# Retention operands stacked by transfers, squares of three heads' norms folded to 64 rows, and the last pair's values taken from the back

## The chip, the cores and the metric

The kernel is written in Bass with the Tile framework and runs on one core of one Trainium2 chip, in one launch. Its metric is the device time in microseconds (us) of one execution. Before the change the median of three runs is 1220.32 us (1220.23 to 1221.1). Beside these there is one profiled execution, which took 1220.88 us; its profile spans 1219.1 us from the first to the last instruction.

The engines named below are PE (TensorE: matmuls and transposes), PEld (its weight loads), ACT (ScalarE), DVE (VectorE), POOL (GpSimd) and SP (SyncE, which here only issues transfers). Each engine runs its own instructions in their written order and waits on semaphores.

## The reference, cut to what matters

Two layers of an encoder over 512 tokens of width 1024, in float32. In each layer:

```
h = RMSNorm(x);  [rq|rk|rv|rg|dq|dk|dv] = h @ w_in
group A, retention, 8 heads of 64:  scores = (q k^T) * decay mask;  o = scores v + cross terms of the recurrent state
         ret = RMSNorm(o per head) * silu(rg)
group B, differential attention, 4 heads of 128:  a = softmax(q1 k1 + alibi) - lam * softmax(q2 k2 + alibi);  da = RMSNorm(a v per head)
x = x + concat(ret, da) @ w_out
x = x + (silu(RMSNorm(x) @ w_gate) * (RMSNorm(x) @ w_up)) @ w_down
```

RMSNorm of a head of group B divides by the root of the mean square over its 128 features; the features lie on the 128 partitions, so this sum runs across partitions and is made by a matmul with a matrix of ones.

## The kernel before, in words

All activations are held with features on partitions and the 512 tokens along the free dimension. A float32 operand is split into a rounded part (`hi`) and the rest (`lo`), both in the type fp32r; a product is then three fp32r matmuls, hi·hi, lo·hi and hi·lo (`mm3`, lines 208 to 210). The cast to `hi` is made by ACT, the subtraction that gives `lo` by DVE.

Each layer has these stages: the first projections (`project_first`, `project_dv`); the four heads of group B, each a generator (`diff_head`), with the remaining projections woven between them as fillers; then group A in four pairs of heads; then the output projection (`project_out`, half 0 for group B, half 1 for group A); then the feed-forward part, most of it in a fast product scheme (`seven`, line 867, from 331 us to 578 us of the span in layer 0), which the change does not touch.

**Group A.** The rows of a pair hold its two heads: partitions 0 to 63 (`ma`) are the first head's 64 features, 64 to 127 (`mb`) the second's. `prepare` (a0 to a3 in `STEPS`) builds, for each head, operands for scores in which both halves of the partitions carry something: `stack_one` makes `q`, with the rounded part on the head's own half and the rest on the other half; `stack_two` makes `khi`, with the rounded part on both halves, and `klo`, with the rest on one half and zeros (a POOL memset) on the other. So one score is two matmuls instead of three (line 536). Engines can write from one half to the other, 64 rows at a time: 2 ACT casts and 2 DVE subtractions for `q` (lines 358, 359), 4 ACT casts and 2 DVE subtractions for `k` (lines 367 to 369). `scores` (b0 to b3) makes the scores and multiplies them with the decays (DVE, line 541), which gives `sm`. `together` (k, v, V) issues a run of plain float32 matmuls: `state` (line 457), `cross` (`o<-wq,rs`, line 469) and `values` (`o<-sm,rv`, line 480). `norm` (n0 to n3) norms the pair and puts its split into `mix`.

**Norms of group B's heads.** `square_sums` squares the head's output (ACT, line 147), splits the squares into hi and lo (lines 226, 227), and issues two matmuls with ones (`aux<-hi,ones_r` line 140, `aux<-lo,ones_r` line 141).

**What sets the order.** `STEPS` is the order in which group A's steps are written; a "-" takes one step of the fillers (projections of the pairs 1 to 3, then the output projection's half 0, which copies each of its banks to `x` on ACT, line 724, and adds the old `x` by an accumulating POOL transfer, line 725). A scheduler then orders each engine's instructions from the written program. Weights come in by SP transfers (line 171) into three buffers; an SP transfer waits in SP's order until its buffer is free. PSUM has eight banks: two each of acc, sc, o and aux.

## Time and profile before

| | |
|---|---|
| median of three runs | 1220.32 us (1220.23 to 1221.1) |
| profiled execution | 1220.88 us, span 1219.1 us |
| PE busy | 1213.1 us, 100% of the span, 7637 matmul records |
| PEld busy | 1084.2 us, 89% |
| DVE busy | 971.3 us, 80% |
| ACT busy | 754.3 us, 62% |
| POOL busy | 93.8 us, 8% |
| granted PE clock | 1.000 |

How to read it: matmuls are pipelined, so a record of PE lasts longer than the time after which the next one starts. A matmul of 512 columns has a record of 0.39 us, while the next starts 0.23 us after it. The price of a matmul is therefore taken from start to start (called its slot below). The same holds for ACT and DVE, whose next instruction can start some 0.1 us before the record of the last one ends.

The stage that the change touches lies between 101 us of the span (the first squares of a head of group B) and some 253 us in layer 0; layer 1 repeats it 604.6 us later.

### The profile page before, as it was taken

How to read it: one execution, taken by the hardware profiler on the slowest of the kernel's cores; microseconds unless marked ns; L12 is line 12 of the kernel's file. 1: busy time of each engine (PE TensorE's matmuls, PEld its weight loads, DVE VectorE, ACT ScalarE, POOL GpSimd, SP SyncE). 2: the span in 40 equal slices, each digit the busy share in tenths (PEclk: the TensorE clock that was granted, in tenths of full speed). 3: DMA queues.
4: the chain of work that ended last, by engine and by line, in shares of the span. 5: the costliest groups of instructions: out<-in, count | busy, mean ns of one | idle time of the engine just before them, and what ended most of it. 6: DMA issues, size and time to landing. Idle time of an engine off the chain costs nothing.

```text
span 1219.1 us, 19925 instructions
## 1 busy us (share of the span) xinstructions
PE 1213.1 (100%) x7637; PEld 1084.2 (89%) x7637; DVE 971.3 (80%) x1601; ACT 754.3 (62%) x1316; POOL 93.8 (8%) x110
## 2 busy tenths in 40 slices
PE   9999999999999999999999999999999999999998
PEld 7888888878899999999888888887888999999997
DVE  6899778868978888886648997786789788898763
ACT  6877777755456656655548776785554565666551
POOL 1000000210011111110000000011100111111100
PEclk9999999999999999999999999999999999999999
DMA  7222221673166786782532222227532767867822
GB/s 267 87 70 74 83 69 53 138 191 104 57 164 166 177 210 158 177 219 90 168 112 79 77 70 70 85 66 163 138 119 67 184 146 188 207 161 181 203 78 95
DMA packets 67839, 158.83 MB, mean 130 GB/s; under 512 B 6176, under 2 KB 16672, under 8 KB 67744
## 3 DMA queue, kind: packets, MB, share of 16 engines
q1 hardware_dynamic: 50864, 127.75, 33.7%
q0 software_dynamic: 16448, 29.36, 14.8%
q8 instruction: 60, 0.98, 0.3%
q10 hardware_dynamic: 432, 0.44, 0.1%
q14 instruction: 35, 0.29, 0.1%
HBM read 153.34 MB, written 4.19 MB: 129 GB/s over the span
## 4 chain that ended last, share of the span: by engine, by line
PE 97%; ACT 2%; issue 0%; DMA 0%; DVE 0%; ACTq 0%
PE acc L867 23%; PE sc L867 17%; PE acc L208 10%; PE acc L209 10%; PE acc L210 10%; PE o L210 3%; PE o L209 3%; PE o L208 3%; PE sc L208 3%; PE sc L210 3%; PE sc L209 3%; PE sc L397 2%; PE o L480 1%; PE aux L413 1%; PE sc L536 1%; PE aux L140 1%
## 5 line engine op out<-in xcount | busy, mean ns | idle before, releaser
L195 ACT CAST hi<-raw 128x1024 fp32r<-128x1024 f32 (+2 forms) x117 | 115.8, 993 | 119.6 <-PE sc L209 39.3
L201 DVE TENSOR_TENSOR lo<-raw,hi 128x1024 fp32r<-128x1024 f32 (+2 forms) x118 | 135.2, 1150 | 45.5 <-ACT hi L195 44.7
L208 PE MATMUL acc<-h,hi 128*128 128x512 f32 (+1 forms) x344 | 133.8, 392 | 0.9 <-ACT h L219 0.9
L209 PE MATMUL acc<-h,hi 128*128 128x512 f32 (+1 forms) x344 | 134.2, 390 | 0.0
L210 PE MATMUL acc<-h,lo 128*128 128x512 f32 (+1 forms) x344 | 133.9, 389 | 0.0
L867 PE MATMUL acc<-hi,hi 128*128 128x256 f32 x432 | 122.5, 284 | 0.0
L867 PE MATMUL acc<-hi,lo 128*128 128x256 f32 x432 | 122.2, 283 | 0.0
L867 PE MATMUL acc<-lo,hi 128*128 128x256 f32 x432 | 122.2, 283 | 0.0
L824 DVE TENSOR_TENSOR lo<-s,hi 128x1024 fp32r<-128x1024 f32 (+1 forms) x78 | 89.0, 1141 | 32.7 <-ACT hi L823 32.4
L824 DVE TENSOR_TENSOR lo<-raw,hi 128x1024 fp32r<-128x1024 f32 (+1 forms) x78 | 89.0, 1141 | 30.5 <-ACT hi L823 26.9
L823 ACT CAST hi<-s 128x1024 fp32r<-128x1024 f32 (+1 forms) x78 | 76.6, 982 | 51.6 <-PE acc L867 37.1
L823 ACT CAST hi<-raw 128x1024 fp32r<-128x1024 f32 (+1 forms) x78 | 76.6, 981 | 39.0 <-PE acc L867 18.8
L867 PEld LDWEIGHTS acc<-lo,hi 128*128 128x128 f32 x432 | 82.9, 192 | 0.1
L867 PEld LDWEIGHTS acc<-hi,hi 128*128 128x128 f32 x432 | 82.9, 192 | 0.1
L867 PEld LDWEIGHTS acc<-hi,lo 128*128 128x128 f32 x432 | 82.9, 192 | 0.0
L208 PEld LDWEIGHTS acc<-h,hi 128*128 128x128 f32 x344 | 64.5, 188 | 15.1 <-ACT h L219 1.0
L210 PEld LDWEIGHTS acc<-h,lo 128*128 128x128 f32 x344 | 64.6, 188 | 13.3
L209 PEld LDWEIGHTS acc<-h,hi 128*128 128x128 f32 x344 | 64.7, 188 | 12.8
L845 POOL DMA_DIRECT2D s<-in_wgu x36 | 43.0, 1195 | 408.3 <-DMA s<-in_wgu 207.0
L867 PE MATMUL sc<-b,s 128*128 128x256 f32 x480 | 69.3, 283 | 0.0
L867 PEld LDWEIGHTS sc<-b,s 128*128 128x128 f32 x480 | 62.8, 192 | 0.0
L107 ACT ACTIVATE sc<-sc,mx 128x512 f32<-128x512 f32 x64 | 46.1, 720 | 20.2 <-DVE mx L401 20.1
(267 smaller groups left out, 3556.3 us busy)
## 6 DMA issues: line engine op xcount, KB each, us to landing
s<-in_wgu SPq DMA_DIRECT2D x54, 512.0 KB, 5.6
s<-in_wgu POOLq DMA_DIRECT2D x36, 512.0 KB, 7.9
raw<-in_wgu SPq DMA_DIRECT2D x34, 512.0 KB, 5.1
raw<-in_wsingle SPq DMA_DIRECT2D x32, 512.0 KB, 3.5
raw<-in_wvv SPq DMA_DIRECT2D x18, 512.0 KB, 3.5
raw<-in_wgu SPq DMA_DIRECT2D x36, 256.0 KB, 3.8
s<-in_wds SPq DMA_DIRECT2D x24, 384.0 KB, 3.4
raw<-in_wout SPq DMA_DIRECT2D x16, 512.0 KB, 4.3
```

Source lines behind the costliest of these rows:

```text
L107: i = nc.scalar.activation(out, src, f, **kw).ins
L140: sums[1] = nc.tensor.matmul(ps, w, hi, start=True, stop=False).ins.name
L195: c = nc.scalar.copy(hi[:, s], raw[:, s])
L201: nc.vector.tensor_tensor(lo[:, s], raw[:, s], f32(hi[:, s]), op=ALU.subtract)
L208: first = nc.tensor.matmul(out, L[0], R[0], start=start, stop=False)
L209: nc.tensor.matmul(out, L[0], R[1], start=False, stop=False)
L210: nc.tensor.matmul(out, L[1], R[0], start=False, stop=stop)
L397: nc.tensor.matmul(ps, q[m][:, t], k[m][part], start=part == 0, stop=part == 1)
L823: last_cast[0] = nc.scalar.copy(hi, raw).ins.name
L824: last_split[0] = nc.vector.tensor_tensor(lo, raw, f32(hi), op=ALU.subtract).ins.name
L845: nc.gpsimd.dma_start(sums, blocks[:, 0::3], accum_op=ALU.add)
L867: mm = nc.tensor.matmul(ps[:, t], L[x1], R[x2], start=start and k + i == 0, stop=k == n // P - 1 and i == 2, skip_group_check=True)
```

## The change

Four edits.

1. **Stacks by transfers.** In `prepare`, `moved_one` and `moved_two` take the place of `stack_one` and `stack_two`. The rounded part and the rest of both heads are made at once on 128 rows; for one of the two operands a cast of 64 rows follows; what has to lie on the other half of the partitions is moved there by SP transfers of 64 rows x 512 (128 KB): two for `q`, three for `k`. Per pair ACT has 4 casts (two of 128 rows, two of 64) instead of 6 of 64 rows, and DVE 2 subtractions of 128 rows instead of 4 of 64. The stacks of group B (`qk_tile`) stay as they were.
2. **Folded squares.** For the heads 0 to 2 of group B, `fold` squares the output and then adds the upper 64 rows onto the lower 64 by an accumulating POOL transfer. After a step of the generator, `folded_sums` rounds the 64 rows (ACT), writes the rest to the other 64 rows of the same tile (DVE), and one matmul with ones sums both. Head 3 keeps `square_sums`. The generator has one step more, and `heads` takes it one filler later.
3. **Values from the back.** The values of pair 3 are written from the last block and the second head to the first block and the first head; `stop` is False on all of them.
4. **Order.** In `STEPS`, b1 stands after k0+k1 instead of after a1, and the first matmul of the run k0+k1 is ordered behind the last score matmul written before it (`scored`).

```diff
@@ -35,7 +35,7 @@
 PLAIN = FFN[0][1]
 BEGUN, LASTS = (2, 9, 10, 20, 21), (18,)
 
-STEPS = "a0 h - b0 - a1 b1 - - - - k0+k1 - - a2 - - a3 V0+v1+k2+k3 b2 b3 n0 n1 - - - V2 n2 - - v3 - n3"
+STEPS = "a0 h - b0 - a1 - - - - k0+k1 b1 - - a2 - - a3 V0+v1+k2+k3 b2 b3 n0 n1 - - - V2 n2 - - v3 - n3"
 
 
 NW, NQK, NMIX, NAH, NHL = 12, 11, 20, 4, 3
@@ -147,6 +147,19 @@
         nc.scalar.activation(sq, src, AF.Square)
         column_sums(ps, w, sq)
         return sq
+
+    def fold(src):
+
+        sq = big("sq")
+        nc.scalar.activation(sq, src, AF.Square)
+        nc.gpsimd.dma_start(sq[:HD], sq[HD:], accum_op=ALU.add)
+        return sq
+
+    def folded_sums(ps, w, sq):
+        parts = big("hl", F32R)
+        nc.scalar.copy(parts[:HD], sq[:HD])
+        nc.vector.tensor_tensor(parts[HD:], sq[:HD], f32(parts[:HD]), op=ALU.subtract)
+        nc.tensor.matmul(ps, w, parts, start=True, stop=True)
 
     def round_ones():
         o = big("ones")
@@ -351,6 +364,28 @@
 
 
         ma, mb = slice(0, HD), slice(HD, P)
+
+        def moved_one(u, tag, bufs):
+            a, b = [big("q", F32R, tag, bufs) for _ in range(2)]
+            lo = big("qlo", F32R)
+            nc.scalar.copy(a, u)
+            nc.vector.tensor_tensor(lo, u, f32(a), op=ALU.subtract)
+            nc.scalar.copy(b[mb], u[mb])
+            nc.sync.dma_start(f32(a[mb]), f32(lo[ma]))
+            nc.sync.dma_start(f32(b[ma]), f32(lo[mb]))
+            return [a, b]
+
+        def moved_two(u, tag, bufs):
+            (ha, la), (hb, lb) = [(big("khi", F32R, tag, bufs), big("klo", F32R, tag, bufs)) for _ in range(2)]
+            nc.gpsimd.memset(f32(lb[ma]), 0.0)
+            nc.scalar.copy(ha, u)
+            nc.vector.tensor_tensor(la, u, f32(ha), op=ALU.subtract)
+            nc.scalar.copy(hb[mb], u[mb])
+            nc.sync.dma_start(f32(hb[ma]), f32(hb[mb]))
+            nc.sync.dma_start(f32(ha[mb]), f32(ha[ma]))
+            nc.sync.dma_start(f32(lb[mb]), f32(la[mb]))
+            nc.gpsimd.memset(f32(la[mb]), 0.0)
+            return [(ha, la), (hb, lb)]
 
         def stack_one(u, tag, bufs):
             q = [big("q", F32R, tag, bufs) for _ in range(2)]
@@ -422,8 +457,14 @@
                     vv = cut(v[hd // 2][j], slice(None), slice((hd % 2) * P, (hd % 2 + 1) * P))
                     mm3(o[:, th * C : (th + 1) * C], vv, (ah[:, j, :], al[:, j, :]), j == 0, j == 3)
                 yield
-            ss = aux_bank()
-            sq = square_sums(ss, consts["ones_r"], o)
+            if hd < DH - 1:
+                sq = fold(o)
+                yield
+                ss = aux_bank()
+                folded_sums(ss, consts["ones_r"], sq)
+            else:
+                ss = aux_bank()
+                sq = square_sums(ss, consts["ones_r"], o)
             rsqrt(sq, ss, 1.0 / P)
             nc.vector.scalar_tensor_tensor(sq, o, gd[:, l : l + 1], sq, op0=ALU.mult, op1=ALU.mult)
             mix[4 + hd] = split(sq, "mix", NMIX)
@@ -438,12 +479,16 @@
             for i, before in zip(ins, [names] + [[i.name] for i in ins]):
                 for name in before:
                     tc.add_manual_dep(i, name, order, reason="one run of plain matmuls")
+            if steps[0][0] == "k":
+                tc.add_manual_dep(ins[0], scored[0], order, reason="one run of plain matmuls")
             run[:] = ins[-1].name, ins[0].name
             first = [ret[int(t[1])]["weigh"] for t in steps if t[0] == "V"][:1]
             for i in first:
                 for name in names:
                     if name != i.name:
                         tc.add_manual_dep(i, name, order, reason="one run of plain matmuls")
+
+        scored = [None]
 
         def state(pr):
             kw, kv, ins = ret[pr]["kw"], aux_bank(), []
@@ -472,9 +517,9 @@
 
         def values(pr):
             o, s, ins = ret[pr]["o"], ret[pr]["s"], []
-            for c in range(2):
+            for c in ((1, 0) if pr == 3 else (0, 1)):
                 for j in range(2):
-                    for hh in range(2):
+                    for hh in ((1, 0) if pr == 3 else (0, 1)):
                         b = slice(hh * HD, (hh + 1) * HD)
                         ins.append(
                             nc.tensor.matmul(
@@ -482,7 +527,7 @@
                                 rv[pr // 2][2 * c + j][:, (pr % 2) * P + hh * HD : (pr % 2) * P + (hh + 1) * HD],
                                 s[c][:, hh, (1 - j) * C : (2 - j) * C],
                                 start=False,
-                                stop=(c == 1 and j == 1),
+                                stop=False,
                                 skip_group_check=True,
                             ).ins
                         )
@@ -509,7 +554,7 @@
                 op=ALU.mult,
             )
             ret[pr].update(qw=qw, kw=kw, state=[i.ins.name])
-            ret[pr]["stacks"] = stack_one(qT, "mix", NMIX), stack_two(kT, "mix", NMIX)
+            ret[pr]["stacks"] = moved_one(qT, "mix", NMIX), moved_two(kT, "mix", NMIX)
 
         def scores(pr):
             lgc = lambda d, hh: lg[:, l * 16 + d * 8 + 2 * pr + hh : l * 16 + d * 8 + 2 * pr + hh + 1]
@@ -536,6 +581,7 @@
                             i = nc.tensor.matmul(out, ks[hh][part][:, sb], qs[hh][:, tb], start=part == 0, stop=part == 1)
                             if run[0]:
                                 tc.add_manual_dep(i.ins, run[0], order, reason="one run of plain matmuls")
+                scored[0] = i.ins.name
                 sm = tpool.tile([P, 2, T], F32, tag="ah", name=nm("sm"), bufs=NAH)
                 for hh in range(2):
                     i = nc.vector.tensor_tensor(
@@ -668,7 +714,7 @@
                 for i in range(4):
                     next(head)
                     yield
-                    if i == 1 and late:
+                    if i in (1, 3) and late:
                         next(late)
                 late = head
             lasthead.append(late)
```

The built order moves at three places of each layer; layer 0 is shown. Numbers behind names are those of buffers.

**ACT, at the casts of the pairs 1 and 2** (q and khi are stacks of a pair, arg and wq its decays, raw and hi a weight and its rounded part, x the copy of an output bank). Before, the last rows of this stretch:

```order
L367 CAST khi_2152<-rk_2063 64x512
L369 CAST khi_2152<-rk_2063 64x512
L195 CAST hi_2505<-raw_2503 128x1024
L724 COPY x_2418<-acc_2405 128x512
L107 ACTIVATE wq_2224<-cst_sb,lg 128x256 x2
```

Behind the change, from pair 1's first cast:

```order
L371 CAST q_1842<-rq_1798 128x512
L373 CAST q_1843<-rq_1798 64x512
L381 CAST khi_1850<-rk_1731 128x512
L567 ACTIVATE arg_2030<-cst_sb,prm_sb 128x384
L567 ACTIVATE arg_2034<-cst_sb,prm_sb 128x384
L107 ACTIVATE wq_2130<-cst_sb,lg 128x256 x2
L383 CAST khi_1852<-rk_1731 64x512
L371 CAST q_2141<-rq_2097 128x512
L373 CAST q_2142<-rq_2097 64x512
L381 CAST khi_2149<-rk_2064 128x512
L770 COPY x_2423<-acc_2410 128x512
```

Before, twelve casts of 64 rows of two pairs and a weight cast stand ahead of the first copy; now there are seven casts, four of them of 128 rows, and decays (arg, wq); the weight cast stands behind the copy.

**PE, at the last pair's values** (o is the pair's bank, wq/rs the cross products, sm the weighted scores, the products with sc the output projection's second half, aux the sums of an earlier pair's norm). Before:

```order
L480 MATMUL o_2525<-sm_2349,rv_1899 64x256 x2
L480 MATMUL o_2525<-sm_2349,rv_1900 64x256 x2
L480 MATMUL o_2525<-sm_2362,rv_1901 64x256
L208 MATMUL sc_2613<-hi_2378,hi_2609 128x512
L209 MATMUL sc_2613<-lo_2379,hi_2609 128x512
L210 MATMUL sc_2613<-hi_2378,lo_2610 128x512
L208 MATMUL sc_2613<-hi_2395,hi_2609 128x512
L209 MATMUL sc_2613<-lo_2396,hi_2609 128x512
L210 MATMUL sc_2613<-hi_2395,lo_2610 128x512
L140 MATMUL aux_2470<-hi_2473,bones_r 128x512
L480 MATMUL o_2525<-sm_2362,rv_1901 64x256
L480 MATMUL o_2525<-sm_2362,rv_1902 64x256 x2
```

Behind the change:

```order
L514 MATMUL o_2530<-wq_2227,rs_373 128x256 x2
L140 MATMUL aux_2475<-hi_2478,bones_r 128x512
L221 MATMUL sc_2618<-hi_2383,hi_2614 128x512
L222 MATMUL sc_2618<-lo_2384,hi_2614 128x512
L223 MATMUL sc_2618<-hi_2383,lo_2615 128x512
L221 MATMUL sc_2618<-hi_2400,hi_2614 128x512
L525 MATMUL o_2530<-sm_2367,rv_1868 64x256 x2
L525 MATMUL o_2530<-sm_2367,rv_1869 64x256 x2
L525 MATMUL o_2530<-sm_2354,rv_1866 64x256 x2
L525 MATMUL o_2530<-sm_2354,rv_1867 64x256 x2
```

Before, the two cross products stood directly ahead of the first row shown, and the values were parted behind the fifth; now all eight stand together, and four products and a sum stand between them and the cross products.

**SP, at the stacks of the pairs 0 and 1.** Before, the loads of the output projection's weights followed each other here without anything between. Behind the change:

```order
L384 DMA khi_1705<-khi_1705 64x512
L385 DMA khi_1703<-khi_1703 64x512
L386 DMA klo_1706<-klo_1704 64x512
L374 DMA q_1695<-qlo_1697 64x512
L375 DMA q_1696<-qlo_1697 64x512
L184 DMA raw_2612<-in_wout 128x1024
L184 DMA raw_2638<-in_wout 128x1024
L374 DMA q_1842<-qlo_1844 64x512
L375 DMA q_1843<-qlo_1844 64x512
L385 DMA khi_1850<-khi_1850 64x512
L384 DMA khi_1852<-khi_1852 64x512
L386 DMA klo_1853<-klo_1851 64x512
```

The transfers of pair 0 and pair 1 stand ahead of and behind two weight loads; those of the pairs 2 and 3 follow, with two more loads between them.

## The prediction

> **What bounds the kernel now.** I read the page first, then the waits of PE, then the stretch around group A in order of time.
>
> The page:
>
> ```profile
> span 1219.1 us, 19925 instructions
> PE 1213.1 (100%) x7637; PEld 1084.2 (89%) x7637; DVE 971.3 (80%) x1601; ACT 754.3 (62%) x1316; POOL 93.8 (8%) x110
> ...
> PE 97%; ACT 2%; issue 0%; DMA 0%; DVE 0%; ACTq 0%
> ```
>
> PE is busy for 1213 of 1219 us and holds 97% of the chain of waits, at full clock (PEclk is 9 in every slice). What an engine beside PE saves is worth nothing unless PE waits for it. The view of PE's waits has three entries, 2.6 us together; the change touches only this one:
>
> ```profile
> PE acc L208 <- ACT x L724: 0.9, 2, 0.5
> ```
>
> So there are three ways to gain: fewer matmuls, that wait, and slots that are longer than they need be.
>
> **The wait.** In order of time, ACT and PE of layer 0, then PE of layer 1:
>
> ```profile
> 202.08 0.62 ACT L226 CAST hi<-sq 128x512 fp32r<-128x512 f32 x1
> 202.60 1.26 ACT L358 CAST q<-rq 64x512 fp32r<-64x512 f32 x2
> 203.88 0.62 ACT L367 CAST khi<-rk 64x512 fp32r<-64x512 f32 x1
> ...
> 206.46 1.26 ACT L358 CAST q<-rq 64x512 fp32r<-64x512 f32 x2
> ...
> 210.31 1.05 ACT L195 CAST hi<-raw 128x1024 fp32r<-128x1024 f32 x1
> 211.27 0.58 ACT L724 COPY x<-acc 128x512 f32<-128x512 f32 x1
> 211.75 0.91 ACT L107 ACTIVATE wq<-cst_sb,lg 128x256 f32<-128x256 f32 x2
> 212.56 1.11 ACT L522 ACTIVATE arg<-cst_sb,prm_sb 128x384 f32<-128x384 f32 x2
> 213.57 1.04 ACT L195 CAST hi<-raw 128x1024 fp32r<-128x1024 f32 x1
> ```
>
> ```profile
> 211.09 0.28 PE L536 MATMUL sc<-q,khi 128*128 128x256 f32 x1
> 211.22 0.28 PE L536 MATMUL sc<-q,klo 128*128 128x256 f32 x1
> 211.90 0.50 PE L208 MATMUL acc<-hi,hi 128*128 128x512 f32 x1 [0.41 <-ACT x L724]
> 212.23 0.39 PE L209 MATMUL acc<-lo,hi 128*128 128x512 f32 x1
> ...
> 815.80 0.28 PE L536 MATMUL sc<-q,klo 128*128 128x256 f32 x1
> 816.54 0.50 PE L208 MATMUL acc<-hi,hi 128*128 128x512 f32 x1 [0.46 <-ACT x L724]
> ```
>
> PE needs a bank that ACT's copy must empty, and the copy stands behind twelve narrow casts of the pairs 1 and 2. A 128-row cast lets the next start after 0.52 us (202.08 to 202.60), a 64-row cast only after 0.64 us (203.88 to 206.46: four in 2.58 us). Layer 0 loses 0.68 less a slot of 0.12 (211.09 to 211.22, rounded), 0.56 us, and 0.10 us more on the next slot (0.33 for 0.23); layer 1 loses 0.74 less 0.12, 0.62 us, and I take the same 0.10.
>
> In the changed order of ACT (shown with the change, from pair 1's casts to the copy that frees the same bank) there stand ahead of the copy four wide casts (2.08), three narrow ones (1.92), the two arg (1.01, from 212.56 to 213.57) and the two wq (0.81, from 211.75 to 212.56): 5.8 us. If this row of casts begins at 202.60 as before, the copy begins at 208.4 instead of 211.27 and ends at 209.0. PE comes to that bank just behind pair 1's first score. That score has 9 matmuls of 512 columns and 4 transposes more ahead of it than before (counted in the order): 9 x 0.23 + 4 x 0.11 = 2.5 us behind this row:
>
> ```profile
> 207.10 0.37 PE L536 MATMUL sc<-q,khi 128*128 128x256 f32 x1
> 207.30 0.60 PE L503 MATMUL aux<-cst_sb,rk 128*128 128x128 f32 x4
> ```
>
> So it starts at 209.6 instead of 207.10. PE asks for the bank at 209.7, which is then free for 0.7 us. First term: -(0.66 + 0.72) = **-1.4 us**; if the copy is as late as ever, 0.
>
> **The folded sums.** Six times one matmul goes. Its slot, from the timeline:
>
> ```profile
> 252.08 0.40 PE L141 MATMUL aux<-lo,bones_r 128*128 128x512 f32 x1
> 252.32 0.39 PE L208 MATMUL acc<-hi,hi 128*128 128x512 f32 x1
> ```
>
> 0.24 us, so 6 x 0.24 = **-1.4 us**; it is sure, since PE streams without a hole there. ACT and DVE have a cast and a subtraction as before. What is added is the accumulating transfer (128 KB), between these two rows of head 1:
>
> ```profile
> 141.62 0.60 ACT L147 ACTIVATE sq<-o 128x512 f32<-128x512 f32 x1 [0.72 <-PE o L210]
> ...
> 147.12 0.40 PE L140 MATMUL aux<-hi,ones_r 128*128 128x512 f32 x1
> ```
>
> The 64-row cast now stands in ACT's order behind one eviction, two weight casts and two exps: some 3.8 us busy; with the idle time that this stretch had (5.5 us from square to sum), 4 to 5 us. Bounds for the transfer are in the table of transfers:
>
> ```profile
> s<-in_wgu POOLq DMA_DIRECT2D x36, 512.0 KB, 7.9
> ...
> raw<-in_wds SPq DMA_DIRECT2D x16, 192.0 KB, 2.6
> ...
> x<-in_xT POOLq DMA_DIRECT2D x8, 256.0 KB, 4.9
> ...
> out_T<-x SPq DMA_DIRECT2D x1, 128.0 KB, 1.7
> ```
>
> Accumulating POOL transfers land after 4.9 us (256 KB) and 7.9 us (512 KB); half the smaller size should be under 4.9, and I take 4. Heads 0 and 2 have more behind the square (ten instructions or more). No cost.
>
> **The last pair's values.** PE's order is shown with the change. The eight values were cut into five and three; now they are whole, and the cut lies behind the two cross products. The times of pair 2 (a whole run) and pair 3:
>
> ```profile
> 239.66 1.03 PE L469 MATMUL o<-wq,rs 128*128 128x256 f32 x4
> 240.61 1.95 PE L480 MATMUL o<-sm,rv 128*64 128x256 f32 x16
> 242.49 0.39 PE L536 MATMUL sc<-q,khi 128*128 128x256 f32 x1
> 242.71 0.28 PE L536 MATMUL sc<-q,klo 128*128 128x256 f32 x1
> ...
> 243.54 1.03 PE L469 MATMUL o<-wq,rs 128*128 128x256 f32 x4
> 244.50 1.51 PE L480 MATMUL o<-sm,rv 128*64 128x256 f32 x10
> 245.94 0.50 PE L208 MATMUL sc<-hi,hi 128*128 128x512 f32 x1
> ...
> 247.43 0.40 PE L140 MATMUL aux<-hi,bones_r 128*128 128x512 f32 x1
> 247.76 1.08 PE L480 MATMUL o<-sm,rv 128*64 128x256 f32 x6
> 248.76 0.50 PE L208 MATMUL sc<-hi,hi 128*128 128x512 f32 x1
> 249.10 0.40 PE L209 MATMUL sc<-lo,hi 128*128 128x512 f32 x1
> ```
>
> Whole: 242.49 - 239.66 = 2.83, and 0.10 on the next slot: 2.93 us. Cut in five and three: 2.40 + 1.00, 0.10 on entering (247.43 to 247.76) and 0.11 on leaving (248.76 to 249.10), taken twice: 3.72 us. The cut costs 0.79 us: two heads' values run side by side (16 records in 1.88 us), and an odd one runs alone. Cut behind the cross products: 0.95 + 0.11, then 0.10 + 1.88 + 0.11 = 3.15 us. Gain 0.57 a layer, both layers **-1.1 us**; between -0.9 (another 0.1 at the new cut) and -1.6 (the new cut free). The Trainium skill (TensorEngine Tiling (Array Packing), Key Properties) says that changing the tiling mode drains the engine, and names no other cause. By it the cross products, which are of full width, would be left for free, and the gain would be 0.68 a layer. The trace does not agree that only the tiling counts: at 207.10 a score of full width takes 0.20 us for 0.12 ahead of transposes of full width, so a change between fp32r and plain float32 costs 0.08 us too.
>
> **The stacks' transfers.** 20 a layer on SP (its order in layer 0 is shown with the change). ACT saves 1.5 us a pair (six narrow casts against two of each kind) and DVE two subtractions, which is worth only the first term. Who may wait for the transfers is PE, at the scores. Pair 0's scores now come behind 46 matmuls of 512 columns, 12 of 256 and 8 transposes more: 12.7 us later, ample. Pair 2's scores come 19.6 us and pair 3's 27.9 us of slots behind pair 1's. Tight is pair 1: its last cast (khi_1852) ends at 202.60 + 0.52 + 0.64 + 0.52 + 1.01 + 0.81 + 0.62 = 206.7, and PE asks for it at 209.6 + 0.12 + 2 x 0.23 = 210.2. The transfer of khi_1850 waits for DVE's subtraction, which I put at about the same time, and PE asks for it at 209.6. So they may take 3.0 us. A store of 128 KB takes 1.7, a load of 192 KB 2.6; I take 2.0, nearest to the row of the same size. At the upper end, 4.9, PE waits 1.9 us a layer, +3.8 us. SP holds weight loads behind these transfers: the loads after pair 0's are read from 213.57 on (above), and go out near 194 by the same sums, so that even 7.9 us of landing leaves 11 us. POOL has 8 narrow memsets a layer as before; pair 1's last one follows its third transfer, and the scores that need it come 3.3 us of slots behind the first.
>
> **Sum.** -1.4 - 1.4 - 1.1 = -3.9 us on 1220.88 us: 1217.0. The median lies 0.6 us under the profiled execution, so the forecast is **1216.4 us**.
>
> **Rivals.**
> - *The wait only moves.* The copy's lead of 0.7 us is small, and another bank's copy or an operand of the pairs 1 to 3 may be late instead. For it: the same ACT order feeds them all. Against: 2.9 us are gained there. Then the first term is 0: 1220.3 - 2.5 = 1217.8.
> - *Pair 1's stacks come late.* Landing 4.9 instead of 2.0: 1216.4 + 3.8 = 1220.2. For it: loads and accumulations in the table are that slow. Against: they read from HBM and are larger.
> - *The folds hold ACT (slower).* ACT takes its instructions in order; if the folded rows land later than the 64-row cast's turn, the exps behind it wait, and PE's transposes behind those. At 7.9 us head 1's cast comes 4 us late and head 2's some 2 us (5.7 us of busy ACT stand behind its square): 6 us a layer, 12 in all if PE feels everything, 6 if half; the kernel is slower once PE feels over 3.2 us a layer. Time 1222.4 to 1228.4, say 1225. Against: 7.9 belongs to 512 KB.
> - *The change doesn't do what it says.* The order shows six matmuls fewer and the values whole; only the stacks could be without effect, which is the first rival.
>
> **Chances.** Forecast 0.60; the wait moves 0.14; pair 1 late 0.18; folds hold ACT 0.08. A measurement of this kernel tells about 0.2% (2.4 us) from no change: under 1217.9 is faster, over 1222.8 slower. Faster: 0.60 and half of the second (1217.8 is at the border) 0.67; slower 0.07, within 0.26. The range goes from 1215.2 (the new cut free, -0.5; two scores a layer no longer stand between transposes, 0.08 us each, -0.3; the rest rounding) to 1220.4 (pair 1 late): it leaves out the slower case and tails.
>
> **What would show it.** Right: PE's waits have no entry on the copy to x; six records of a single `hl,ones_r` matmul; the last values as 16 records in 1.9 us; stack transfers near 2 us. Wrong: a wait of PE at pair 1's scores on a transfer, idle time of ACT in front of the 64-row cast `hl` ended by a transfer, or new gaps of PE on DVE at pair 3.

## The result, and the profile after

The changed kernel takes **1216.57 us** in the median of six runs (1216.24 to 1216.87), the kernel before 1220.41 us (1220.23 to 1221.1) beside it. The ratio is 0.9967, 95% interval 0.9956 to 0.9978: faster by 3.8 us. The forecast was 1216.4 us.

The page of the changed kernel and the view of PE's waits (line, what it waited for: us, times, longest):

```profile
span 1214.5 us, 19995 instructions
PE 1210.0 (100%) x7631; PEld 1083.2 (89%) x7631; DVE 961.1 (79%) x1585; ACT 744.8 (61%) x1300; POOL 99.2 (8%) x116
```

```profile
PE aux L118 <- PEq L1165: 0.8, 1, 0.8
PE acc L221 <- ACT h L232: 0.4, 1, 0.4
```

PE has six records fewer, 7631, and its wait on the copy to `x` is gone. What is left lies in the start-up, as before. PE still is the bound: 1210.0 of 1214.5 us.

ACT and PE of the changed kernel in order of time, around the copy to `x` (L770 here):

```profile
200.52 1.06 ACT L208 CAST hi<-raw 128x1024 fp32r<-128x1024 f32 x1 [1.82 <-PE acc L222]
...
201.99 0.62 ACT L371 CAST q<-rq 128x512 fp32r<-128x512 f32 x1
...
208.20 0.58 ACT L770 COPY x<-acc 128x512 f32<-128x512 f32 x1
...
210.29 1.04 ACT L208 CAST hi<-raw 128x1024 fp32r<-128x1024 f32 x1
...
208.25 1.03 PE L548 MATMUL aux<-cst_sb,rk 128*128 128x128 f32 x8
209.04 0.36 PE L581 MATMUL sc<-q,khi 128*128 128x256 f32 x1
209.24 0.40 PE L221 MATMUL acc<-hi,hi 128*128 128x512 f32 x1
```

The copy begins at 208.20, right behind the last cast ahead of it, and ends at 208.78; PE takes the bank at 209.24. The order of casts worked out ahead of the run gave 208.4, 209.0 and 209.7.

One thing about this order was said wrongly with the change. The weight cast that stood between the narrow casts and the copy (at 210.31 before) does not stand behind the copy now. Counted in ACT's order it is the 35th of 195 weight casts (`hi<-raw`) in both kernels, and in the changed kernel the 35th is the row at 200.52, ahead of pair 1's casts, which begin no later for it (201.99, for 202.60 before). The row behind the copy, at 210.29, is the 36th, which stood behind the copy before too (213.57). So the row of ACT from pair 1's first cast to the copy is 208.20 - 201.99 = 6.2 us for 211.27 - 202.60 = 8.7 us before, and 0.96 us of the difference is this weight cast.

The last pair, in the same kernel's order of time on PE:

```profile
241.72 1.03 PE L514 MATMUL o<-wq,rs 128*128 128x256 f32 x4
242.40 0.58 PE L140 MATMUL aux<-hi,bones_r 128*128 128x512 f32 x1
242.82 0.39 PE L221 MATMUL sc<-hi,hi 128*128 128x512 f32 x1
...
243.83 1.95 PE L525 MATMUL o<-sm,rv 128*64 128x256 f32 x16
245.71 0.50 PE L221 MATMUL sc<-hi,hi 128*128 128x512 f32 x1
...
247.91 0.40 PE L140 MATMUL aux<-hi,bones_r 128*128 128x512 f32 x1
```

The eight values (16 records) run whole in 1.88 us. From the cross products to the sum of the last norm (the second L140) PE does the same work as before, both with 14 matmuls of 512 columns between: 247.91 - 241.72 = 6.19 us, where the kernel before took 250.47 - 243.54 = 6.93 us. That is 0.74 us a layer.

The table of transfers of the changed kernel (KB each, median us from issue to landing):

```profile
khi<-khi SPq DMA_DIRECT2D x16, 128.0 KB, 3.0
q<-qlo SPq DMA_DIRECT2D x16, 128.0 KB, 4.1
klo<-klo SPq DMA_DIRECT2D x8, 128.0 KB, 3.6
sq<-sq POOLq DMA_DIRECT2D x6, 128.0 KB, 2.9
```

The stacks' transfers take 3.0 to 4.1 us, not 2.0; the accumulating one 2.9, not 4.

Where the time went, by PE's records: "layer 0" runs from the first projected product to the first product of the feed-forward part with seven products, "layer 1" from there to the same product of layer 1. In the profiled executions of before they take 325.21 and 604.64 us, of after 323.11 and 602.77: -2.10 and -1.87. The start-up is 0.46 us shorter (6.04 to 5.58), the end 0.16, together 4.6 us of span. The medians differ by 3.8 only; the start-up comes back below.

### The profile page after: what moved, and what is told of

Same layout as the page of the kernel before. It is cut to its first block, busy times and chain, and to the rows that moved or that the text cites. A ratio compares the mean times of both kernels' runs of the same rounds, so it can differ in the third digit from the quotient of the medians.

```text
span 1214.5 us, 19995 instructions
## 1 busy us (share of the span) xinstructions
PE 1210.0 (100%) x7631; PEld 1083.2 (89%) x7631; DVE 961.1 (79%) x1585; ACT 744.8 (61%) x1300; POOL 99.2 (8%) x116
## 4 chain that ended last, share of the span: by engine, by line
PE 99%; DMA 0%; ACT 0%; DVE 0%; issue 0%
PE acc L913 23%; PE sc L913 17%; PE acc L221 11%; PE acc L222 11%; PE acc L223 11%; PE o L223 3%; PE o L222 3%; PE o L221 3%; PE sc L221 3%; PE sc L222 3%; PE sc L223 3%; PE sc L432 2%; PE sc L581 1%; PE o L525 1%; PE aux L448 1%; PE aux L140 1%
```

## The experiments

The intervals of the ratios are some 0.1% wide to each side, over 1 us, and most parts are worth no more than that. So each kernel is read by its two stages against those of before, and by the rows that changed; the medians are given beside them.

**One part alone.** The kernel before with one edit each.

`back_only`, the values from the back:

```diff
-            for c in range(2):
+            for c in ((1, 0) if pr == 3 else (0, 1)):
                 for j in range(2):
-                    for hh in range(2):
+                    for hh in ((1, 0) if pr == 3 else (0, 1)):
...
-                                stop=(c == 1 and j == 1),
+                                stop=False,
```

> The kernel before with the last pair's values from the back alone; stacks, norms and the order of steps as before. The built order has the two cross products, seven fp32r matmuls, then the eight values whole, in both layers; all else as before. Theory of the prediction (new cut at 0.11 + 0.10 a layer): 0.57 us a layer, 1220.4 - 1.1 = 1219.3. New cut almost free, as the trace of the changed kernel shows it (crosses 0.68 + 0.19 + 0.09, values 1.88 + 0.11): 0.77 a layer, 1220.4 - 1.5 = 1218.9. Rival, that the end of the values was hidden by DVE or ACT work and the gain comes back behind it: 1220.4. The wait of PE on ACT's copy to x (0.9, 2 times) stays under all three.

Measured: 1220.32 us beside 1220.7, ratio 0.9997 (0.9989 to 1.0006); stages -0.15 and -0.12. The rival is right: nearly all of the gain comes back. A new entry in PE's waits and the place in layer 0:

```profile
PE aux L140 <- ACT hi L226: 0.7, 2, 0.4
```

```profile
243.35 1.03 PE L469 MATMUL o<-wq,rs 128*128 128x256 f32 x4
...
249.31 0.40 PE L210 MATMUL sc<-hi,lo 128*128 128x512 f32 x1
250.06 0.50 PE L140 MATMUL aux<-hi,bones_r 128*128 128x512 f32 x1 [0.36 <-ACT hi L226]
250.40 0.39 PE L208 MATMUL acc<-hi,hi 128*128 128x512 f32 x1
```

Up to the sum PE would need 6.19 us, as in the changed kernel. But the slot from 249.31 to 250.06 is 0.52 us too long, the next one 0.10. So 0.62 of 0.74 us goes back. The sum waits for ACT's cast of the squares. ACT in this kernel, then in the changed kernel:

```profile
247.93 0.60 ACT L147 ACTIVATE sq<-o 128x512 f32<-128x512 f32 x1 [4.26 <-PE o L480]
248.82 0.69 ACT L107 ACTIVATE sq<-aux,eps_sb 128x512 f32<-128x512 f32 x1 [0.29 <-PE aux L141]
249.40 0.61 ACT L226 CAST hi<-sq 128x512 fp32r<-128x512 f32 x1
```

```profile
245.83 0.60 ACT L147 ACTIVATE sq<-o 128x512 f32<-128x512 f32 x1 [3.34 <-PE o L525]
246.46 0.62 ACT L239 CAST hi<-sq 128x512 fp32r<-128x512 f32 x1
```

In `back_only` alone a step of the earlier pair's norm (`sq<-aux`), which itself waits for PE's sum, stands between the square and its cast, so the cast ends at 250.01. In the changed kernel the cast follows the square and ends at 247.08, 0.83 us before PE needs it. An estimate from these rows: with the changed kernel's order the cast would end 1.25 us behind the square's start, at 249.18, and PE asks at 249.54, so the gain would have stayed. The number of matmuls between the values and the sum (seven here, nine there) is not what decides.

`fold_only`, the folded sums:

```diff
-            ss = aux_bank()
-            sq = square_sums(ss, consts["ones_r"], o)
+            if hd < DH - 1:
+                sq = fold(o)
+                yield
+                ss = aux_bank()
+                folded_sums(ss, consts["ones_r"], sq)
+            else:
+                ss = aux_bank()
+                sq = square_sums(ss, consts["ones_r"], o)
...
-                    if i == 1 and late:
+                    if i in (1, 3) and late:
```

> The kernel before with the folded sums of three heads alone. Its built order differs in two more places: the weight cast of 1024 columns that stood between the twelve narrow casts and the copy to x now stands behind the copy (about 0.96 us earlier for the copy), and PE comes to the copy's bank behind all eight scores of pair 1; and the last pair's values are cut in 4, 1 and 3 in place of 5 and 3 (one cut more, some 0.2 us a layer, +0.4). Theory A, the one of the prediction (the number of narrow casts makes the copy late, only the moved stacks remove the wait): six slots of 0.24 less, the wait stays, 1220.4 - 1.4 + 0.4 = 1219.4. Rival B (the wait was due to the place of that weight cast and of the scores, which the fold moves): 1220.4 - 1.4 - 1.4 + 0.4 = 1218.0, and PE's waits have no entry on the copy to x. Rival C (the folds hold ACT): 1220.4 or more, with ACT idle ahead of the cast hl.

Measured: 1219.11 us beside 1220.7, ratio 0.9988 (0.9979 to 0.9997); stages -0.74 and -0.61. PE's waits have no entry on the copy to `x` (L743 here). ACT, then PE at that place, then PE at the last pair:

```profile
200.86 1.05 ACT L208 CAST hi<-raw 128x1024 fp32r<-128x1024 f32 x1
...
209.93 0.57 ACT L743 COPY x<-acc 128x512 f32<-128x512 f32 x1
210.53 1.05 ACT L208 CAST hi<-raw 128x1024 fp32r<-128x1024 f32 x1
...
210.29 0.28 PE L555 MATMUL sc<-q,klo 128*128 128x256 f32 x1
210.56 0.50 PE L221 MATMUL acc<-hi,hi 128*128 128x512 f32 x1
...
243.23 1.08 PE L499 MATMUL o<-sm,rv 128*64 128x256 f32 x8
...
244.68 0.65 PE L499 MATMUL o<-sm,rv 128*64 128x256 f32 x2
...
246.40 1.08 PE L499 MATMUL o<-sm,rv 128*64 128x256 f32 x6
```

Twelve narrow casts still stand ahead of the copy, and PE still is not held by an amount that counts: the copy ends at 210.50, PE asks at 210.41, and the slot is 0.27 us for 0.12, the next one 0.10 too long: 0.25 us lost instead of 0.66. Rival B is right on the wait: not the moved stacks alone take it away, the fold does too, by what it does to the order. But the weight cast did not go behind the copy, as the expectation reads the order: it is the row at 200.86, ahead of the narrow casts, and the one behind the copy is the next weight's. With the 0.96 us put back ahead of the copy, the copy would end at 211.46, 1.05 us after PE asks (an estimate from these rows). The rival's price for the cut was too low: 4, 1 and 3 cost 249.59 - 242.28 = 7.31 us up to the next sum, 0.38 us more than 5 and 3.

`moved_only`, the stacks by transfers:

```diff
-            ret[pr]["stacks"] = stack_one(qT, "mix", NMIX), stack_two(kT, "mix", NMIX)
+            ret[pr]["stacks"] = moved_one(qT, "mix", NMIX), moved_two(kT, "mix", NMIX)
```

> The kernel before with the stacks by transfers alone. In its built order pair 1's scores come ten fp32r matmuls later than in the changed kernel, and the last pair's values are cut in 4, 1 and 3 (+0.4). Theory: the wait goes, 1220.4 - 1.4 + 0.4 = 1219.4, and the scores never wait for a transfer since they come later. Rival (transfers of 3.0 to 4.1 us are late somewhere, for pair 0 or pair 1): 1220.4 or more and an entry of PE on a queue or idle PE ahead of a score.

Measured: 1219.91 us beside 1220.7, ratio 0.9995 (0.9986 to 1.0004); stages -0.23 and -0.30. No wait on the copy, none on a transfer; the last values are cut in 4, 1 and 3, again 7.31 us. The rows at the copy (L746 here):

```profile
209.09 0.58 ACT L746 COPY x<-acc 128x512 f32<-128x512 f32 x1
...
210.48 0.48 PE L208 MATMUL acc<-hi,hi 128*128 128x512 f32 x1
```

The copy ends 0.8 us ahead of PE. The wait goes, as the theory has it; 0.38 us a layer of its gain goes to the third cut. But here too the weight cast has moved ahead of the row of casts (to 201.93): with its 0.96 us put back, the copy would end 0.15 us after PE asks. No run has the moved stacks with this cast in its old place, so how much of the wait the shorter stacks take away by themselves is an estimate only.

The order of steps alone (edit 4 on the kernel before) was not run: PE's and ACT's built orders are then the same as before in every row. Taken out of the changed kernel, it does alter PE's order; this was not run either, and its share there stays open.

**One order on ACT.** Was it the amount of ACT's work or the place of one cast? `cast_behind` was meant to be the kernel before with that weight cast behind the copy:

```diff
-    for t in chunk(wout[l, half, m // 2])]
+    for t in chunk(wout[l, half, m // 2], after=copied[0] if half == 0 and m == 2 else None)]
...
-                    nc.scalar.copy(x[m], ps[m])
+                    copied[0] = nc.scalar.copy(x[m], ps[m]).ins.name if m == 0 else copied[0]
+                    if m:
+                        nc.scalar.copy(x[m], ps[m])
```

> The kernel before with one order among ACT's instructions: the weight cast of 1024 columns that stands between the twelve narrow casts and the copy to x goes behind this copy; twelve narrow casts, the old stacks, the unfolded sums and the values from the front stay, and PE has the same matmuls ahead of that bank. Theory A, the prediction's (the narrow casts make the copy late): the copy stays too late, 1220.4 with PE's entry of 0.9 us on it. Rival B (one weight cast of 0.96 us too many ahead of the copy; any edit that takes a microsecond from ACT there or brings PE later removes the wait): the copy begins near 210.3 and ends near 210.9, PE asks at 211.3, no entry; 0.66 us in layer 0 and 0.72 in layer 1, 1219.1. If the weight cast is then late for the next four products, 1220.4 with a new entry of PE on a cast.

Measured: 1224.59 us beside 1220.57, ratio 1.0031 (1.0020 to 1.0042); stages +1.66 and +3.01. PE's waits:

```profile
PE sc L536 <- DVE sm L541: 1.3, 2, 0.7
PE acc L208 <- ACT hi L195: 0.9, 2, 0.5
```

ACT behind the copy, and PE at the bank:

```profile
209.94 0.57 ACT L724 COPY x<-acc 128x512 f32<-128x512 f32 x1
210.54 2.00 ACT L195 CAST hi<-raw 128x1024 fp32r<-128x1024 f32 x2
...
211.64 0.50 PE L208 MATMUL acc<-hi,hi 128*128 128x512 f32 x1 [0.40 <-ACT hi L195]
```

This run does not answer the question. The edit holds back the cast for the products of `m == 2`, the 34th weight cast, which before is made at 195.50, far ahead of the narrow casts; the 35th, which stood between them and the copy, then comes behind it too (two casts from 210.54 on). The products of `m == 2` are the very ones that take the bank, so the wait on the cast, 0.9 us, and another entry of 0.8 us on DVE's subtraction behind it are made by the edit. The entries named come to 3.0 of the 4.7 us by which the two stages grew; the rest, and the wait of 1.3 us on DVE's products with the decays, are not traced further. What the run does show is the copy: with twelve narrow casts and no weight cast behind them it begins at 209.94 for 211.27 and ends at 210.51, while PE asks at 211.09. The entry on the copy is gone, as rival B said. `fold_only` is the better test: the same twelve casts, the weight cast ahead of them and not behind, and 0.25 us of the wait left.

**One part undone.** The changed kernel with one edit taken back. `un_stacks` (the inverse of the diff of `moved_only`):

> The changed kernel with the old stacks of six narrow casts a pair; fold, values from the back and order of steps stay. Theory A (the narrow casts make the copy late): the wait comes back, 1216.6 + 1.4 = 1218.0, and PE's waits name the copy to x again, or pair 1's scores wait for ACT's narrow casts. Rival B (the wait went since the fold put the weight cast behind the copy): 1216.6, or 0.2 less since the 0.24 us by which pair 1's first score waits in layer 1 goes too; the transfers would then buy nothing.

Measured: 1217.47 us beside 1220.7, ratio 0.9972 (0.9961 to 0.9983); stages -1.85 and -1.74. At the copy:

```profile
210.02 0.57 ACT L770 COPY x<-acc 128x512 f32<-128x512 f32 x1
...
210.65 0.50 PE L221 MATMUL acc<-hi,hi 128*128 128x512 f32 x1
```

As in `fold_only`, 0.25 us is left of the wait. Beside the other edits the twenty transfers a layer are worth 0.1 to 0.4 us (against the two traces of the changed kernel, -2.10 and -1.87, -2.08 and -2.13), not 0.7: between the two, nearer to B. The weight cast stands ahead of the narrow casts here too (200.94).

`un_fold` (the inverse of the diff of `fold_only`):

> The changed kernel with the column sums of the three heads in two matmuls again. Six slots of 0.24 more: 1216.6 + 1.4 = 1218.0, and no wait of PE on the copy to x, since the moved stacks alone are enough for it. If the wait is gone only because the fold moves the weight cast behind the copy, it comes back: 1219.4 and an entry of PE on ACT at the copy to x.

Measured: 1217.49 us beside 1220.56, ratio 0.9975 (0.9966 to 0.9985); stages -1.32 and -1.44, no wait on the copy. Against the changed kernel's second trace that is 0.76 and 0.69 us a layer, three slots, as expected.

`un_back` (the inverse of the diff of `back_only`):

> The changed kernel with the last pair's values from the front again; its built order is that of the changed kernel but for the end of pair 3, where the values are cut in 4, 1 and 3. By the prediction's price of the cut (5 and 3 against whole: 0.57 a layer): 1216.6 + 1.1 = 1217.7. By the two runs with the same cut in 4, 1 and 3 (7.31 us from the cross products to the second following sum, against 6.19 whole: 1.12 a layer): 1216.6 + 2.2 = 1218.8. If the sum of pair 3's norm waited in the changed kernel anyway, as it does when the values alone are turned: under 1217.0.

Measured: 1218.33 us beside 1220.56, ratio 0.9981 (0.9972 to 0.9990); stages -1.00 and -1.05, the values in 4, 1 and 3 and 249.43 - 242.14 = 7.29 us up to the sum. The second case: here the edit is worth 1.1 us a layer, alone it was worth 0.12.

**The account.** Four amounts a layer, each read from rows above, make the seven kernels: the wait (0.66 us in before, 0.25 with the old stacks and the fold), three slots of the fold (0.72), the cut in 5 and 3 (0.74 above the changed kernel's) or in 4, 1 and 3 (1.12 above it), and the wait of the last norm (0.62).

| against before, us a layer | worked out | layer 0 | layer 1 |
|---|---|---|---|
| `back_only` | -0.74 + 0.62 = -0.12 | -0.15 | -0.12 |
| `fold_only` | -0.72 - 0.41 + 0.38 = -0.75 | -0.74 | -0.61 |
| `moved_only` | -0.66 + 0.38 = -0.28 | -0.23 | -0.30 |
| `un_stacks` | -0.72 - 0.74 - 0.41 = -1.87 | -1.85 | -1.74 |
| `un_fold` | -0.66 - 0.74 = -1.40 | -1.32 | -1.44 |
| `un_back` | -0.72 - 0.66 + 0.38 = -1.00 | -1.00 | -1.05 |
| changed kernel, two traces | -0.72 - 0.66 - 0.74 = -2.12 | -2.10, -2.08 | -1.87, -2.13 |

The three edits alone sum to -1.12 in layer 0, together they give -2.10. Two overlap (with either of them the weight cast moves and most of the wait goes), and the third needs the others: alone it is given back at the norm, by the order of two ACT instructions, and without it each of the others pays for a third piece of the values.

**The changed kernel again**, `after_again`:

> The changed kernel once more, for a second trace and for medians beside the others on one chip. Start-up: the first product begins at 5.6 us in the changed kernel's trace and at 6.0 in the trace of before; two groups of values (5.5 to 5.6 and 5.9 to 6.2) are found over all traces of this case. If this is a matter of the execution and not of the change, the second trace may show 6.0; the stages of the two layers should come again within 0.2 us each, the median at 1216.6.

Measured: 1216.12 us beside 1220.48, ratio 0.9964 (0.9951 to 0.9976). Layer 1 differs from the first trace by 0.26 us, at pair 1's first score. First trace, then second:

```profile
810.75 1.03 PE L548 MATMUL aux<-cst_sb,rk 128*128 128x128 f32 x8
811.79 0.36 PE L581 MATMUL sc<-q,khi 128*128 128x256 f32 x1
```

```profile
810.66 1.03 PE L548 MATMUL aux<-cst_sb,rk 128*128 128x128 f32 x8
811.45 0.36 PE L581 MATMUL sc<-q,khi 128*128 128x256 f32 x1
```

1.04 us against 0.79: in the first execution the score came 0.25 us late, in the second not at all. In layer 1 the score has no slack, and the landing decides. The difference from before is 4.4 us in this call, 3.8 in the first. The start-up was 5.46 us; values from 5.46 to 6.25 are found over these kernels (6.25 in `early_h` and `hop_khi`, which do not differ from the changed kernel up to there), so I don't count its 0.46 us as the change's. What sets it stays open.

**The price of a late transfer.** `hop_khi` sends one operand of pair 1 over a further buffer:

```diff
             nc.sync.dma_start(f32(hb[ma]), f32(hb[mb]))
-            nc.sync.dma_start(f32(ha[mb]), f32(ha[ma]))
+            nc.sync.dma_start(via[ma], f32(ha[ma]))
+            nc.sync.dma_start(f32(ha[mb]), via[ma])
```

> The changed kernel with one transfer of pair 1's keys sent by way of a further buffer (two transfers in a row in place of one), so that this one operand lands later; the rest as in the changed kernel but for places of a few casts. Theory: pair 1's first score has no slack left (3.0 us of landing were allowed and 3.0 measured), so each us of landing is a us of PE. The second transfer can be issued when the first has landed, near 207.1 in place of 205.9 in layer 0, and about as much later in layer 1: 1.2 us a layer, 1216.6 + 2.4 = 1219.0, with idle PE at pair 1's first score ended by the transfer. If the score had slack: 1216.6. If both landings count in full: up to 1222.6.

Measured: 1219.46 us beside 1220.48, ratio 0.9994 (0.9985 to 1.0003); 3.3 us above the changed kernel of the same call. PE's waits, the second transfer's issue on SP, and the score:

```profile
PE sc L595 <- DMA khi<-via: 2.7, 2, 1.5
```

```profile
209.27 0.46 SPq L399 DMA_DIRECT2D khi<-via  x1
...
211.64 0.48 PE L595 MATMUL sc<-q,khi 128*128 128x256 f32 x2 [1.50 <-DMA khi<-via]
```

The second transfer was issued at 209.27, later than the 207.1 expected, and released the score 2.4 us later. 2.7 of the 3.3 us are this wait by name. So the rival of late stacks had a real place and its price was about right: what lands late there is paid by PE.

**More of the same.** Three kernels fold further. `four_folds` folds head 3 too:

```diff
-            if hd < DH - 1:
-                sq = fold(o)
...
+            sq = fold(o)
...
-STEPS = "a0 h - b0 - a1 - - - - k0+k1 b1 - - a2 ...
+STEPS = "a0 h - h b0 - a1 - - - - k0+k1 b1 - - a2 ...
```

> The changed kernel with the fourth head folded too (its fold one step of the order earlier, its sum where it was). If a fold is hidden behind other work here as well: two slots of 0.24 less, 1216.6 - 0.5 = 1216.1, and two scores a layer no longer stand between fp32 transposes. If the last head's transfer (2.9 us) is late for its sum, or pair 1's scores, which now stand directly behind the eight transposes, come before their transfers: 1216.6 to 1219, with idle PE at the sum or at pair 1's first score.

Measured: 1221.06 us beside 1220.56, ratio 1.0004 (0.9996 to 1.0013); stages +1.70 and -0.07. The second case, and dearer than the 1219 it allowed, at pair 1's scores, which are in one row behind the transposes here:

```profile
PE sc L577 <- ACT q L373: 1.9, 2, 1.0
```

Two more entries, 0.9 us each, name POOL's zeros in `klo` and the transfer of `khi`.

`early_h` has the same fold with the steps `h a0 - h b0`:

> The changed kernel with the fourth head folded too, now with its fold one step earlier in the table (h a0 - h b0 where three folds have a0 h - b0). In its built order pair 1's eight scores stand in one row twelve matmuls of 512 columns (2.8 us) behind the eight transposes, where the changed kernel has the first score directly behind them; the end of pair 3 and ACT's casts ahead of the copy to x are as in the changed kernel. If the loss of the first kernel with four folds came only from the place of pair 1's scores (3.7 us of waits on their operands): two slots of 0.24 less and no wait of 0.2 us in layer 1, 1216.6 - 0.7 = 1215.9. If the fourth head's transfer itself is late for its sum: 1217 or more, with idle PE at the matmul with hl.

Measured: 1217.3 us beside 1220.48, ratio 0.9972 (0.9961 to 0.9982); stages -1.84 and -1.46, 1.2 us slower than the changed kernel of the same call. Most of the loss of `four_folds` did come from the place of the scores, since with twelve matmuls between the waits on their operands are gone. But now PE asks for the copy's bank directly behind the transposes and waits there (0.2 us by the view) and, in layer 1, for DVE too (0.2 us). From start to start these places cost some 0.4 us in layer 0 and 0.8 in layer 1, more than the two slots saved. The matmul with `hl` did not wait, so neither expected case holds as it was put.

`qk_folds` folds the late q and k projections' squares from 64 to 32 rows a head (for these, `fold_halves` with two accumulating transfers stands for the square, and a single matmul with `bones_r` for the two):

> The changed kernel with the squares of the two late q and the two late k projections folded too, each head's 64 rows to 32 by two accumulating transfers, so that one matmul with the same block of ones sums both parts: eight matmuls less in the two layers, two accumulating transfers and one 32-row subtraction more for each. If the transfers are hidden: 8 x 0.24 = 1.9, 1216.6 - 1.9 = 1214.7. If the later q and k make the scores of heads 2 and 3 late, or POOL's queue (16 more transfers) holds the heads' folds: 1216.6 or more, with PE idle ahead of a score or of a folded sum. The copy to x stands two exponentials and a cast later in ACT's order here (1.7 us), so the wait of 0.7 us a layer may come back: 1216.1.

Measured: 1219.35 us beside 1220.56, ratio 0.9991 (0.9982 to 0.9999); stages -1.10 and +0.03, so 1.0 and 1.9 to 2.2 us worse than the changed kernel, though four slots a layer went.

```profile
PE sc L451 <- DVE mx L455: 2.5, 2, 1.4
PE sc L600 <- ACT x L789: 1.7, 1, 1.7
```

```profile
814.62 0.48 PE L600 MATMUL sc<-q,khi 128*128 128x256 f32 x2 [1.72 <-ACT x L789]
```

The second case. The banks of the heads' scores are read late by DVE. The other wait is at pair 1's first score in layer 1. The view names the copy to `x`, but that copy ended at 814.20, and the score reads `q` and `khi`: the transfer of `khi` issued at 810.77 landed at 814.53, just ahead of the score, so it is again a late stack and not the copy's bank. No kernel here beats the changed one.

## Why the prediction was right, step by step

- **The bound.** Right. PE's busy time sets the end; only slots and waits of PE moved it.
- **The wait, -1.4 us.** Right in its size and its place: the entry is gone. The cause was read too narrowly. "The copy stands behind twelve narrow casts" named one part of ACT's row as the reason and left out the weight cast of 0.96 us that stood between them and the copy. With the twelve casts in place and this one moved ahead (`fold_only`, `un_stacks`) the wait falls to 0.25 us; put back in the changed kernel, it would end the copy at 209.74, 0.6 us after PE asks at 209.16 (an estimate from the rows above). In every kernel here that lost this wait, the weight cast had left its place; why the scheduler moves it is open. The sum came out because it was added up from the new order, in which the cast was gone. I gave the whole of -1.4 us to the stacks; beside the fold they are worth 0.1 to 0.4 us a layer. That the copy came at 208.20 for 208.4 is partly luck: the row took 6.2 us and not 5.8, and began 0.6 us earlier. Two wide casts let the next start only after 0.65 us (201.99 to 202.64 and 206.38 to 207.03 in the changed kernel), and a narrow one in `fold_only` let the copy start after 0.52 (209.41 to 209.93), so the price of 0.52 for wide and 0.64 for narrow casts is not a matter of width alone.
- **The folded sums, -1.4 us.** Right: `un_fold` gains 1.32 and 1.44 us where the changed kernel's second trace has 2.08 and 2.13, 0.76 and 0.69 us a layer for 0.72. The accumulating transfer took 2.9 us in the median for the 4 assumed (5.1 at most), and ACT never waited for it; the rival that the folds hold ACT did not happen.
- **The values, -1.1 us.** The sign was right and the size too small: 0.74 us a layer for 0.57. The mis-sized term is the price of the new cut, 0.22 us. One half, 0.11 on leaving the cross products, is not there: from 241.72 to 242.82 two cross products and a sum take 1.10 us, what four records of 0.22 and a sum of 0.23 take by themselves. The other half was counted twice: the 0.95 us of the cross products already held the step into the values (their last slot is 0.31 for 0.22), and 0.10 on entering was added again. Since the old cut cost 0.79 us and 0.74 were gained, the whole new cut costs 0.05 us at most. The Trainium skill (TensorEngine Tiling (Array Packing), Key Properties) has it that a change of tiling mode drains the engine; by it the cross products are left for free and the gain is 0.68. The rows agree with it here, and my reason against it was a misreading. A score directly behind transposes does have a slot of 0.20 us for 0.12, but the last transpose ahead of it has one of 0.03 for 0.11 (207.07 to 207.10 to 207.30 in the kernel before); together they are 0.23 us, what a transpose and a score cost anyway. So the 0.08 us a score, also taken for the lower end of the range, is nothing. I also took the kernel before as the only comparison: with the other edits made and this one not, the values would lie in three pieces (`un_back`), so it earns 1.1 us a layer there.
- **The transfers, 2.0 us.** Wrong by half to double: 3.0, 3.6 and 4.1 us. The row of the same size that I chose was one store to HBM, 1.7 us; the stacks' transfers go from SBUF to SBUF, five in a row. Which of the two makes them longer, no run separates: the second transfer of `hop_khi`, also from SBUF to SBUF, had landed within 2.4 us of its issue. The allowance of 3.0 us for pair 1 was right, and in layer 1 it was just used up: 0.25 us late in one execution, in time in another, and 1.5 and 1.2 us late with one hop more.
- **The rivals.** "The wait only moves" did not happen in the changed kernel. "Pair 1's stacks come late" was the nearest miss. "Without effect" was half true of the stacks, in a way I had not put: the fold too moves the weight cast, and with it most of their wait is gone already.
- **The sum.** -3.9 us was forecast and -3.8 measured, with two errors that nearly cancel in the profile: 0.4 us more from the values, and up to 0.3 us of late score. The start-up, 0.46 us in the first trace, moves the profiled execution and not the account.

## What to carry to other kernels

Edits on one bound engine are not added up from their separate prices: two that remove the same wait count once, and one whose gain ends at the next late operand counts only when that operand comes in time. So price each both alone on the old kernel and undone on the new one, and check in the built order what a scheduler moved elsewhere, since an edit can remove a wait or cut a run that it doesn't touch. Both surprises here hang on the place of one ACT instruction: a weight cast ahead of the narrow casts in place of behind them, and a step of another norm between a square and its cast. So when an engine seems short by a microsecond in a stretch, look first for an instruction there that could be done earlier, without making what follows late; and before a run is read as a test of such an order, check in its trace that the instruction meant is the one that moved.

## What the runs showed of the hardware that was not expected

- A transfer of 64 rows x 512 from SBUF to SBUF took 3.0 to 4.1 us from issue to landing on SP's queue, in the medians, longer than a store of the same size to HBM in the kernel before (1.7 us); the accumulating one on POOL's queue took 2.9. The same transfer varied enough between two executions to make a matmul 0.25 us late in one of them.
- The last pair's values, two heads side by side, cost by the number of pieces and by odd ones left alone: whole 6.19 us up to the next sum, in 5 and 3 6.93 us, in 4, 1 and 3 7.31 us, for the same matmuls.
- A run of plain float32 matmuls at full width was cut from fp32r matmuls for 0.05 us at most, and transposes in plain float32 and scores in fp32r followed each other for nothing (0.03 + 0.20 us for 0.11 + 0.12), where a change to half width and back costs 0.10 to 0.11 us a side.
